# A fixed order for the opening of a hybrid decoder layer: one k-tile first, first modulation on TensorE, a closing norm over three engines

## The chip, the core and the metric

The kernel runs on one core of one Trainium2 chip. The metric is the device time of one execution in microseconds. The engines are TensorE (PE, its weight loads PEld), VectorE (DVE), ScalarE (ACT), GpSimd (POOL) and SyncE (SP), which issues most transfers.

## What is computed

x is 256 tokens by 2048 channels, float32; c is one conditioning vector. The reference, cut:

```
mod = silu(c) @ w_ada + b_ada            # w_ada 2048 x 6144
shift, scale, gate = split(mod, 3)
h = layer_norm(x) * (1 + scale) + shift
proj = h @ w_in                          # 2048 x 9280
q_lat, kv_lat, mla_gate, pool_in, pool_gate, gate_logits = split(proj)
y_mla = (mla(q_lat, kv_lat) * silu(mla_gate)) @ w_mla_o
y_pool = (pool(pool_in) * silu(pool_gate)) @ w_pool_o
g_mla, g_pool = split(sigmoid(gate_logits + b_gates), 2)
y = (g_mla * y_mla + g_pool * y_pool) @ w_out
out = layer_norm(ALPHA * x + (1 + gate) * y, ln_g, ln_b)
```

The first layer norm has no weights. No product with w_in can start before the shift and the scale of its 128 input channels are known, and each of these is a sum over all 2048 rows of w_ada.

## The kernel before

Products keep float32 accuracy by splitting both operands: hi is the operand rounded by a ScalarE copy, lo the rest, subtracted on VectorE (`split`, lines 92 to 94), and a block's product is three matmuls, hi by hi, lo by hi and hi by lo (`mm3t`, lines 104 to 106). Weights arrive as raw tiles of up to 1 MB (five buffers, `RAWB`) and are converted into hi/lo pairs of 128x1024 (four pairs, `HB`). A job is one such pair and its matmuls: two k-tiles of 128 channels for one block of 512 columns and both halves of the tokens, 12 matmuls of 512 columns. `execute` writes the jobs out in order, with conversions up to four pairs ahead; a planner (the tile framework's scheduler) then orders the instructions of each engine by priority and by its own estimate of when they are ready, and sets the waits.

The 2048 channels are 16 k-tiles. w_in has 18 blocks of 512 columns for the token-major branches (qkv 2, pi 2, pg 2, gp 4, mg 4, gm 4). It is worked through in four groups of k-tiles, `KGROUPS`: 2, 4, 4 and 6. In each group all blocks get their partial product; the first group's is copied from PSUM by ScalarE (line 453), later ones are added by VectorE to the stored tile (line 455). One exception, `early_jobs`: the qkv blocks take k-tiles 0 and 1 one after the other, as soon as each is modulated.

The modulations (`ada_jobs`) stand between these jobs, placed by `weave` over the first 85% of a group. For a set of k-tiles, VectorE multiplies each of 16 slices of w_ada by a column of silu(c) and sums (`accumulate`, lines 323 and 325); TensorE then folds the 128 partitions by a product with a column of ones (line 350), VectorE adds the bias (354, 357), ScalarE applies shift and scale to the normalised, transposed x (363) and splits it into hh and hl. The sets are 1, 1, 2, 2, 4, 2 and 4 k-tiles. A sum over one k-tile has 128x256 steps, over two 128x512, over four 128x1024.

At the start x (2 MB) is loaded, its statistics taken on VectorE (406), it is normalised by ScalarE (423), transposed by TensorE (432) and copied back (435). At the end, the last block of the last projection is done for the first 128 tokens, then for the others in two halves of 256 columns (`out_mm`, 955 to 957), each followed by `residual` on VectorE (930 to 933). `closing_norm` centres four pieces of 512 columns on VectorE (940); for the first tokens ScalarE scales and GpSimd adds the bias (945, 946), for the last ones VectorE does both in one step (948).

Of the kernel before, what the change touches and what calls it, by code (L numbers as in the profile page):

```python
# [15 lines left out]
P = 128  # L16
# [21 lines left out]
SPL = 0  # L38
# [19 lines left out]
KGROUPS = ((0, 2), (2, 4), (6, 4), (10, 6))  # L58
# [3 lines left out]
def hybrid_layer(  # L62
# [222 lines left out]
    vT = const.tile([P, 80], F32, name="vT")  # L285
    VB_ADA, VB_G, VB_PS, VB_Q, VB_KV = 0, 32, 64, 72, 76

    def load_vecs():
        for o, n, src in (
            (VB_ADA, 32, b_ada[0, 0:2 * D]), (VB_G, 32, b_gates[0]), (VB_PS, 8, pool_scale[0]),  # L290
            (VB_Q, 4, q_norm_g[0]), (VB_KV, 4, kv_norm_g[0]),
        ):
            nc.sync.dma_start(vecs[o:o + n, :], src.rearrange("(r q) -> r q", q=P))
# [22 lines left out]
    def accumulate(accs, raw, per, ui):  # L316
        w = accs[0].shape[1]
        for i in range(per):
            t = ui * per + i
            src = raw[:, i * w:(i + 1) * w]  # L320
            acc = accs[t % len(accs)]
            if t < len(accs):
                V.tensor_scalar(acc, src, s_c[:, t:t + 1], None, op0=ALU.mult)
            else:
                V.scalar_tensor_tensor(acc, src, s_c[:, t:t + 1], acc, op0=ALU.mult, op1=ALU.add)  # L325

    def ada_jobs(k0, nk):
# [5 lines left out]
        def unit(raw, ui):  # L333
            if ui == 0:
                acc = ck(shape=(P, 1024), name="acc") if nk > 2 else wk(512, "acc")
                accs.extend(acc[:, o * 2 * ncol:(o + 1) * 2 * ncol] for o in range(2 if nk == 1 else 1))
            accumulate(accs, raw, per, ui)
# [8 lines left out]
        def finish():  # L346
            pa = bank()
            for j in range(2 * nk):
                for i, acc in enumerate(accs):
                    T.matmul(  # L350
                        pa[:, j:j + 1], lhsT=acc[:, j * P:(j + 1) * P], rhs=ones[:, 0:1], start=i == 0,
                        stop=i == len(accs) - 1,
                    )
            V.tensor_tensor(
                mod_shift[:, k0:k0 + nk], pa[:, 0:nk], vT[:, VB_ADA + k0:VB_ADA + k0 + nk], op=ALU.add,
            )
            V.scalar_tensor_tensor(
                mod_scale[:, k0:k0 + nk], pa[:, nk:2 * nk], 1.0,
                vT[:, VB_ADA + KT + k0:VB_ADA + KT + k0 + nk], op0=ALU.add, op1=ALU.add,
            )  # L360
# [17 lines left out]
    def rstd_steps(dst, var, eps, ve, t):  # L378
        def a():
            V.tensor_scalar(ve, var, eps, None, op0=ALU.add)  # L380
            A.activation(t, ve, AF.Sqrt)
            V.reciprocal(dst, t)
# [16 lines left out]
    norms = []  # L399

    def input_norm():
        load_vecs()
        for t in range(2):
            st = work.tile([P, 4, 6], F32, tag="bns", name="bns")
            for j in range(4):
                V.bn_stats(st[:, j, :], xt[2 * t + j // 2][:, (j % 2) * 512:(j % 2 + 1) * 512])
            mu, rs = ln_stats(st)
            nmr = work.tile([P, 1], F32, tag="nmr", name="nmr")
            V.tensor_scalar(nmr, mu, rs, -1.0, op0=ALU.mult, op1=ALU.mult)
            norms.append((rs, nmr))  # L410
        normalize(0)
        pv = bank()
        T.transpose(pv[:, :P], vecs, ident)
        A.copy(vT, pv[:, :80])
        to_features(0, 2)
        normalize(1)
        to_features(2, 4)

    def normalize(j):
        for t in range(2):  # L420
            rs, nmr = norms[t]
            xx = xt[2 * t + j]
            A.activation(xx, xx, AF.Identity, scale=rs, bias=nmr)

    def to_features(q0, q1):
        for q in range(q0, q1):
            nT.append(ck(name="nT"))
            for t in range(2):
                pt = bank()
                for j in range(4):  # L430
                    k = q * 4 + j
                    T.transpose(
                        pt[:, j * P:(j + 1) * P], xt[2 * t + k // 8][:, (k % 8) * P:(k % 8 + 1) * P], ident,
                    )
                A.copy(nT[q][:, :, t * P:(t + 1) * P], pt.rearrange("p (j n) -> p j n", j=4))
# [42 lines left out]
    def early_jobs(name):  # L478
        banks = []

        def fn(wh, wl, k):
            if k == 0:
                banks.extend(bank() for _ in range(4))
            xh, xl = hsl(hh, k), hsl(hl, k)
            for t in range(2):
                ts = slice(t * P, (t + 1) * P)
                for cb in range(2):
                    cs = slice(cb * CB, (cb + 1) * CB)
                    mm3t(banks[2 * t + cb], xh[:, ts], xl[:, ts], wh[:, 0, cs], wl[:, 0, cs], k == 0, k == 1)
# [366 lines left out]
    def gate_jobs(cb):  # L856
        accs = []

        def unit(raw, ui):
# [3 lines left out]
            accumulate(accs[:1], raw, 4, ui)  # L863
# [71 lines left out]
    def closing_norm(t):  # L935
        mu, rs = ln_stats(fin["s"][t])
        order = (0, 1, 2, 3)
        for j in order:
            uc = fin["u"][t][j // 2][:, j % 2, :]
            V.scalar_tensor_tensor(uc, uc, mu, fin["g"][j // 2][:, j % 2, :], op0=ALU.subtract, op1=ALU.mult)  # L940
        for j in order:
            uc = fin["u"][t][j // 2][:, j % 2, :]
            bc = fin["b"][j // 2][:, j % 2, :]
            if t == 0 or j < SPL:
                A.activation(uc, uc, AF.Copy, scale=rs)
                G.tensor_tensor(uc, uc, bc, op=ALU.add)
            else:
                V.scalar_tensor_tensor(uc, uc, rs, bc, op0=ALU.mult, op1=ALU.add)
            nc.sync.dma_start(out[t * P:(t + 1) * P, j * 512:(j + 1) * 512], uc)
# [9 lines left out]
    def out_jobs(cb):  # L959
# [3 lines left out]
        def fn(wh, wl, kc, kh):  # L963
# [10 lines left out]
            if last:  # L974
                residual(0, cb, banks[0])
                if cb < 3:
                    residual(1, cb, banks[1])
                else:
                    closing_norm(0)
                    for q in range(2):  # L980
# [121 lines left out]
```

## Time and profile before

| | |
|---|---|
| median of 3 runs | 803.99 us (803.51 to 804.83) |
| the profiled execution's own time | 803.81 us |
| its span, first to last instruction | 802.0 us |
| TensorE busy | 767.5 us (96%) |
| VectorE busy | 649.7 us (81%) |
| ScalarE busy | 422.7 us (53%) |
| moved by DMA | 195.41 MB |

The span leaves out what lies around the instructions, 1.8 us here. Matmuls are pipelined, so a busy TensorE counts overlapping instructions once; start-to-start times tell its rate. The clock granted to TensorE is given as a share of full speed: 1.00 or 0.50 at a moment, in between as a mean over a stretch.

### The profile page before, as it was taken

Reading aid. Unit: us, or ns where it says so; the run is one execution under the profiler, and the core shown is the slowest. Engines: PE = TensorE matmul, PEld = TensorE weight load, DVE = VectorE, ACT = ScalarE, POOL = GpSimd, SP = SyncE. Lnnn points to the kernel's source line nnn. Section 1 sums busy time; section 2 is a strip of 40 time slices with the busy share of each in tenths; the row PEclk is TensorE's granted clock in tenths of the full one; section 3 lists DMA queues with packets and bytes.
Section 4 is the critical chain, followed back from the end, with each engine's and each line's share of the span. In section 5 each row is a group of like instructions: output and inputs, shape, how many; then the busy total and the mean of one; then the engine's idle time right before and its main releaser. Section 6 shows DMA issues by size and latency. Waiting matters only on the chain.

```text
span 802.0 us, 10653 instructions
## 1 busy us (share of the span) xinstructions
PE 767.5 (96%) x3985; PEld 658.6 (82%) x3985; DVE 649.7 (81%) x977; ACT 422.7 (53%) x588; POOL 12.0 (2%) x51
## 2 busy tenths in 40 slices
PE   2699999999999999999999999999999999999993
PEld 2588888888888888888888999999998888888883
DVE  6978798979998886678978769887776899769855
ACT  5467643353433556565665676666664344443611
POOL 1000000000000000000100000000000000000002
PEclk9799999999999999999999999999999999999997
DMA  9999998968998666645766646556454979789502
GB/s 284 328 309 363 375 354 299 343 214 280 332 343 300 218 216 198 208 132 178 256 222 188 193 145 197 200 196 200 161 196 121 318 272 343 266 323 362 206 2 105
DMA packets 112989, 195.41 MB, mean 244 GB/s; under 512 B 6484, under 2 KB 32292, under 8 KB 112936
## 3 DMA queue, kind: packets, MB, share of 16 engines
q1 hardware_dynamic: 112296, 192.62, 71.4%
q0 software_dynamic: 640, 2.10, 0.9%
q8 instruction: 31, 0.51, 0.3%
q14 instruction: 22, 0.18, 0.1%
HBM read 192.60 MB, written 2.10 MB: 243 GB/s over the span
## 4 chain that ended last, share of the span: by engine, by line
PE 94%; DMA 3%; DVE 2%; SPq 1%; ACT 0%; issue 0%; DVEq 0%; ACTq 0%
PE ps L104 22%; PE ps L106 22%; PE ps L105 22%; PE ps L957 4%; PE ps L956 4%; PE ps L955 4%; PE ps L98 2%; PE ps L97 2%; PE ps L99 2%; PE ps L260 2%; PE ps L832 1%; DMA raw<-in_w_ada_dram 1%; PE ps L759 1%; PE ps L758 1%; PE ps L760 1%; DMA raw<-in_w_in_dram 1%
## 5 line engine op out<-in xcount | busy, mean ns | idle before, releaser
L93 ACT ACTIVATE hi<-raw 128x1024 fp32r<-128x1024 f32 (+1 forms) x256 | 267.0, 1044 | 299.5 <-PE ps L105 201.5
L94 DVE TENSOR_TENSOR lo<-raw,hi 128x1024 fp32r<-128x1024 f32 x254 | 304.8, 1203 | 82.2 <-ACT hi L93 81.6
L104 PE MATMUL ps<-hi,hh 128*128 128x512 f32 x576 | 225.9, 396 | 4.8 <-ACT hh L93 3.6
L105 PE MATMUL ps<-hi,hl 128*128 128x512 f32 x576 | 225.9, 392 | 0.0
L106 PE MATMUL ps<-lo,hh 128*128 128x512 f32 x576 | 221.8, 392 | 0.0
L325 DVE SCALAR_TENSOR_TENSOR acc<-raw,s_c,acc 128x512 f32<-128x512 f32 (+2 forms) x163 | 128.5, 798 | 16.8 <-DMA raw<-in_w_ada_dram 15.0
L104 PEld LDWEIGHTS ps<-hi,hh 128*128 128x128 f32 x576 | 109.4, 190 | 27.4 <-ACT hh L93 3.8
L106 PEld LDWEIGHTS ps<-lo,hh 128*128 128x128 f32 x576 | 109.2, 190 | 23.0
L105 PEld LDWEIGHTS ps<-hi,hl 128*128 128x128 f32 x576 | 109.3, 190 | 22.7 <-DVE hl L94 0.4
L104 PE MATMUL ps<-hi,zh 128*128 128x512 f32 x128 | 50.2, 397 | 0.0
L105 PE MATMUL ps<-hi,zl 128*128 128x512 f32 x128 | 50.2, 392 | 0.0
L106 PE MATMUL ps<-lo,zh 128*128 128x512 f32 x128 | 49.4, 391 | 0.0
L97 PE MATMUL ps<-cn_h,hi 128*128 128x256 f32 x160 | 46.0, 288 | 0.0
L98 PE MATMUL ps<-cn_l,hi 128*128 128x256 f32 x160 | 45.2, 283 | 0.0
L99 PE MATMUL ps<-cn_h,lo 128*128 128x256 f32 x160 | 45.2, 283 | 0.0
L957 PE MATMUL ps<-hi,ml 128*128 128x512 f32 (+1 forms) x120 | 45.1, 376 | 0.0
L956 PE MATMUL ps<-lo,mh 128*128 128x512 f32 (+1 forms) x120 | 45.0, 375 | 0.0
L955 PE MATMUL ps<-hi,mh 128*128 128x512 f32 (+1 forms) x120 | 44.9, 376 | 0.0
L98 PEld LDWEIGHTS ps<-cn_l,hi 128*128 128x128 f32 x160 | 30.6, 191 | 0.1
L97 PEld LDWEIGHTS ps<-cn_h,hi 128*128 128x128 f32 x160 | 30.6, 191 | 0.1
L99 PEld LDWEIGHTS ps<-cn_h,lo 128*128 128x128 f32 x160 | 30.6, 191 | 0.0
L106 PEld LDWEIGHTS ps<-lo,zh 128*128 128x128 f32 x128 | 24.0, 188 | 5.1
(211 smaller groups left out, 991.8 us busy)
## 6 DMA issues: line engine op xcount, KB each, us to landing
raw<-in_w_in_dram SPq DMA_DIRECT2D x55, 1024.0 KB, 5.8
raw<-in_w_ada_dram SPq DMA_DIRECT2D x64, 512.0 KB, 6.5
raw<-in_w_in_dram SPq DMA_DIRECT2D x35, 512.0 KB, 3.8
raw<-in_w_ada_dram SPq DMA_DIRECT2D x16, 1024.0 KB, 5.8
raw<-in_w_mla_o_dram SPq DMA_DIRECT2D x16, 1024.0 KB, 5.2
raw<-in_w_out_dram SPq DMA_DIRECT2D x16, 1024.0 KB, 5.7
raw<-in_w_kv_b_dram SPq DMA_DIRECT2D x8, 1024.0 KB, 5.4
raw<-in_w_pool_o_dram SPq DMA_DIRECT2D x8, 1024.0 KB, 5.0
```

Of the source, the lines that this page charges most:

```text
L93: A.activation(hi, src, AF.Copy)
L94: V.tensor_tensor(lo, src, hi.bitcast(F32), op=ALU.subtract)
L97: T.matmul(ps, lhsT=wh, rhs=xh, start=first, stop=False, skip_group_check=True)
L98: T.matmul(ps, lhsT=wh, rhs=xl, start=False, stop=False, skip_group_check=True)
L99: T.matmul(ps, lhsT=wl, rhs=xh, start=False, stop=last, skip_group_check=True)
L104: T.matmul(ps, lhsT=xh, rhs=wh, start=first, stop=False, skip_group_check=True)
L105: T.matmul(ps, lhsT=xl, rhs=wh, start=False, stop=False, skip_group_check=True)
L106: T.matmul(ps, lhsT=xh, rhs=wl, start=False, stop=last, skip_group_check=True)
L325: V.scalar_tensor_tensor(acc, src, s_c[:, t:t + 1], acc, op0=ALU.mult, op1=ALU.add)
L955: T.matmul(ps, lhsT=xh, rhs=wh[:, k, :], start=first and k == 0, stop=False)
L956: T.matmul(ps, lhsT=xh, rhs=wl[:, k, :], start=False, stop=False)
L957: T.matmul(ps, lhsT=xl, rhs=wh[:, k, :], start=False, stop=last and k == 1)
```

## The change

Way in. `way_in` replaces `input_norm`, `early_jobs` and the first two modulations, and together with the jobs of the first k-group it runs under `manual_schedule`, in which TensorE, VectorE, ScalarE and SyncE keep the order of the program. The sum for k-tile 0 is done on TensorE: for 13 of the 16 slices of w_ada, `direct` uses the slice as stationary operand and one column of silu(c) as the moving one; slices 3, 7 and 11 stay on VectorE. For k-tile 1, slices 0 to 13 are on VectorE, 14 and 15 on TensorE. Eight blocks (qkv, pi, pg and the first two of gp) take k-tile 0 alone, in four pairs; qkv keeps its four PSUM banks until k-tile 1 is modulated, the others are copied out. The transposes of x stand between the products of `direct`. Normalising is split between ScalarE and VectorE. Four small loads go out from ScalarE instead of five from SyncE.

k-groups. After that: ten blocks take k-tiles 0 and 1; then six take 1 to 3 and twelve 2 and 3; then all 18 take 4 to 7; then all take 8 to 15. The modulation sets are 2, 4, and 4 and 4, woven into the first three of these.

End. The first tokens' closing norm is wholly on VectorE. Of the last tokens' first piece, 448 columns are made on TensorE as three products added in PSUM: the identity by the bias, a diagonal of the root by the residual (already multiplied by the weight), a diagonal of minus mean times root by the weight. ScalarE copies it out. VectorE's steps go piece by piece, one of them between the root's request and its use; the end is under `manual_schedule` for VectorE and ScalarE.

The diff, cut:

```diff
+TE = 448
-KGROUPS = ((0, 2), (2, 4), (6, 4), (10, 6))
...
+            nc.scalar.dma_start(vecs[o:o + n, :], src.rearrange("(r q) -> r q", q=P))
...
+    def fold(pa, acc, first, last):
+        n = acc.shape[1] // P
+        for j in range(n):
+            T.matmul(pa[:, j:j + 1], lhsT=acc[:, j * P:(j + 1) * P], rhs=ones[:, 0:1], start=first and j == 0,
+                     stop=last, skip_group_check=True)
...
-            V.tensor_tensor(t, dst, dst, op=ALU.mult)
-            V.tensor_tensor(t, t, ve, op=ALU.mult)
+                V.scalar_tensor_tensor(t, dst, dst, ve, op0=ALU.mult, op1=ALU.mult)
...
+        def direct(pa, r, t, first, last):
+            for j in range(2):
+                T.matmul(pa[:, j:j + 1], lhsT=r[:, t % 8, j, :], rhs=s_c[:, t:t + 1], start=first and j == 0,
+                         stop=last, skip_group_check=True)
+        def apply(k, pa):
+            modulation(pa, k, 1)
+            h = wk(S, "h")
+            A.activation(hsl(hh, k), hsl(nT, k), AF.Identity, scale=mod_scale[:, k:k + 1], bias=mod_shift[:, k:k + 1])
+            V.tensor_scalar(h, hsl(nT, k), mod_scale[:, k:k + 1], mod_shift[:, k:k + 1], op0=ALU.mult, op1=ALU.add)
+            V.tensor_tensor(hsl(hl, k), h, hsl(hh, k).bitcast(F32), op=ALU.subtract)
+        def product(pair, k, banks, first, last):
+            xh, xl = hsl(hh, k), hsl(hl, k)
+            for cb in range(2):
+                cs = slice(cb * CB, (cb + 1) * CB)
+                for t in range(2):
+                    ts = slice(t * P, (t + 1) * P)
+                    mm3t(banks[2 * cb + t], xh[:, ts], xl[:, ts], pair[0][:, cs], pair[1][:, cs], first, last)
...
+        load_vecs()
+        w_q = w_load(0, OFFS["qkv"], 2 * CB)
+        r0 = [ada_load(0, u) for u in range(2)]
+        w_p = w_load(0, OFFS["pi"], 4 * CB)
+        w_g = w_load(0, OFFS["gp"], 2 * CB)
+        r1 = [ada_load(1, 0)]
+        w_q1 = w_load(1, OFFS["qkv"], 2 * CB)
+        r1.append(ada_load(1, 1))
...
+        to_features(0)
+        pq = convert(w_q)
...
+        pa, acc = bank(), wk(2 * P, "acc")
+        for t in range(16):
+            if t in (4, 8, 12):
+                to_features(t // 4)
+            if t == 12:
+                fold(pa, acc, False, False)
+            if t in (3, 7, 11):
+                accumulate(acc, r0[t // 8][:, t % 8].rearrange("p s n -> p (s n)"), t, t == 3)
+            else:
+                direct(pa, r0[t // 8], t, t == 0, t == 15)
+        apply(0, pa)
+        pp = [convert(w_p[:, i * HALF:(i + 1) * HALF]) for i in range(2)]
+        bq = [bank() for _ in range(4)]
+        product(pq, 0, bq, True, False)
+        pg = convert(w_g)
+        for pair, name in ((pp[0], "pi"), (pp[1], "pg"), (pg, "gp")):
+            banks = [bank() for _ in range(4)]
+            product(pair, 0, banks, True, True)
+            if name == "pg":
+                accumulate_1(0, 8)
+                pq = convert(w_q1)
+            evict(name, 0, banks)
+        accumulate_1(8, 14)
+        pa = bank()
+        fold(pa, acc, True, False)
+        for t in (14, 15):
+            direct(pa, r1[1], t, False, t == 15)
+        apply(1, pa)
+        product(pq, 1, bq, False, True)
+        evict("qkv", 0, bq)
...
+    def closing_norm_1():
+        V.bn_aggr(mv[:, 0:2], fin["s"][1].rearrange("p a b -> p (a b)"))
+        a, b = rstd_steps(rs, mv[:, 1:2], LN_EPS, ve, t)
+        T.matmul(ps[:, :TE], lhsT=ident, rhs=part("b", 1, 0, 0, TE), start=True, stop=False, skip_group_check=True)
+        a(lambda: centre(1, 1, mu))
+        b()
+        V.tensor_scalar(nmr, mu, rs, -1.0, op0=ALU.mult, op1=ALU.mult)
+        for i, (sc, src) in enumerate(((rs, "u"), (nmr, "g"))):
+            d = dg[:, i * P:(i + 1) * P]
+            A.activation(d, ident, AF.Copy, scale=sc)
+            T.matmul(ps[:, :TE], lhsT=d, rhs=part(src, 1, 0, 0, TE), start=False, stop=i == 1, skip_group_check=True)
+        A.copy(part("u", 1, 0, 0, TE), ps[:, :TE])
+        put(1, 0, 0, TE)
+        close(1, 1, rs)
+        for j, c0 in ((2, 0), (3, 0), (0, TE)):
+            centre(1, j, mu, c0)
+            close(1, j, rs, c0)
...
+    fixed = tc.manual_schedule(engines={getattr(mybir.EngineType, e) for e in ("PE", "DVE", "Activation", "SP")})
+    fixed.__enter__()
+    way_in()
+    names = ("pi", "pg", "gp", "qkv", "mg", "gm")
+    ahead = (("pi", 0), ("pi", 1), ("pg", 0), ("pg", 1), ("gp", 0), ("gp", 1))
+    def groups(n, cb):
+        if (n, cb) in ahead:
+            return None, (1, 3), (4, 4), (8, 8)
+        return None if n == "qkv" else (0, 2), (2, 2), (4, 4), (8, 8)
+    ADA = (((2, 2),), ((4, 4),), ((8, 4), (12, 4)))
...
+        if gi == 0:
+            main += todo(lambda: fixed.__exit__(None, None, None), rope_load)
```

## Rows read from the trace of the kernel before

**Rows 1.** The page's first part: busy us, share, instructions.

```profile
PE 767.5 (96%) x3985; PEld 658.6 (82%) x3985; DVE 649.7 (81%) x977; ACT 422.7 (53%) x588; POOL 12.0 (2%) x51
```

**Rows 2.** Busy time by stretch: length, PE, PEld, DVE, ACT, POOL, clock, DMA share, GB/s.

```profile
38.00:84.00 46.00, 46.00 (x199) 38.05 (x200) 37.64 (x49) 33.32 (x53) 1.23 (x2) 0.94 1.00 343
84.00:186.00 102.00, 102.00 (x459) 84.74 (x458) 89.92 (x100) 45.42 (x50) 0.00 (x0) 1.00 0.88 308
186.00:286.00 100.00, 100.00 (x454) 83.20 (x454) 91.89 (x110) 43.02 (x44) 0.54 (x1) 1.00 0.87 297
```

**Rows 3.** Waits of TensorE, whole execution: us in total, times, longest.

```profile
PE ps L104 <- ACT hh L93: 3.6, 1, 3.6
```

**Rows 4.** Timeline of TensorE in the stream: start, length; twelfth product after the first.

```profile
774.65 0.39 PE L955 MATMUL ps<-hi,mh 128*128 128x512 f32 x1
...
777.15 0.39 PE L957 MATMUL ps<-hi,ml 128*128 128x512 f32 x1
```

**Rows 5.** Timeline of TensorE, way in: start, length of the merged row.

```profile
13.64 1.12 PE L432 MATMUL ps<-ident,x 128*128 128x128 f32 x4 [2.21 <-ACT x L423]
16.66 4.79 PE L432 MATMUL ps<-ident,x 128*128 128x128 f32 x28 [1.90 <-ACT x L423]
21.30 0.95 PE L350 MATMUL ps<-ones,acc 128*128 128x1 f32 x8
25.80 1.40 PE L104 MATMUL ps<-hi,hh 128*128 128x512 f32 x4 [3.55 <-ACT hh L93]
...
35.35 1.27 PE L350 MATMUL ps<-ones,acc 128*128 128x1 f32 x6
...
42.75 0.63 PE L105 MATMUL ps<-hi,hl 128*128 128x512 f32 x1
...
43.60 0.45 PE L105 MATMUL ps<-hi,hl 128*128 128x512 f32 x1
```

**Rows 6.** Timeline of VectorE and ScalarE, way in.

```profile
17.74 3.25 DVE L325 SCALAR_TENSOR_TENSOR acc<-raw,s_c,acc 128x256 f32<-128x256 f32 x8 [0.43 <-DMA raw<-in_w_ada_dram]
...
25.33 0.42 ACT L93 ACTIVATE hh<-nT 128x256 fp32r<-128x256 f32 x1
...
28.86 1.06 ACT L93 ACTIVATE hi<-raw 128x1024 fp32r<-128x1024 f32 x1 [3.11 <-DMA raw<-in_w_in_dram]
...
46.25 0.59 ACT L494 COPY qkv<-ps 128x512 f32<-128x512 f32 x1
```

**Rows 7.** Timeline of VectorE while its queue is full.

```profile
63.61 3.10 DVE L325 SCALAR_TENSOR_TENSOR acc<-raw,s_c,acc 128x512 f32<-128x512 f32 x4
66.63 1.22 DVE L94 TENSOR_TENSOR lo<-raw,hi 128x1024 fp32r<-128x1024 f32 x1
...
103.82 1.28 DVE L455 TENSOR_TENSOR pi<-ps,pi 128x512 f32<-128x512 f32 x2
105.02 1.21 DVE L94 TENSOR_TENSOR lo<-raw,hi 128x1024 fp32r<-128x1024 f32 x1
106.15 1.27 DVE L325 SCALAR_TENSOR_TENSOR acc<-raw,s_c,acc 128x1024 f32<-128x1024 f32 x1
107.35 1.21 DVE L94 TENSOR_TENSOR lo<-raw,hi 128x1024 fp32r<-128x1024 f32 x1
```

**Rows 8.** Waits from 186 to 260 us: us in total, times, longest.

```profile
ACT hi L93 <- PE ps L105: 43.3, 26, 2.3
```

**Rows 9.** Timeline: a float32 product in attention, then the end.

```profile
494.70 0.83 PE L832 MATMUL ps<-vn,pT 128*128 128x128 f32 x6
...
783.79 0.42 DVE L932 SCALAR_TENSOR_TENSOR ua<-ua,tmp 128x256 f32<-128x256 f32 x1
...
788.77 0.28 PE L957 MATMUL ps<-hi,ml 128*128 128x256 f32 x1
...
789.54 1.52 DVE L932 SCALAR_TENSOR_TENSOR ua<-ua,tmp 128x256 f32<-128x256 f32 x1
...
795.55 2.74 DVE L948 SCALAR_TENSOR_TENSOR ua<-ua,mv,lb 128x512 f32<-128x512 f32 x4
```

More of the change, by code (lines that the diff above doesn't have):

```diff
@@ L37 @@
 NW = 8
-SPL = 0
+TE = 448
 WA = (0.0, 0.0, 0.0, 0.0)
@@ L314, in hybrid_layer, with accumulate, accumulate_raw, modulation @@
     nT, hh, hl = [], [], []
-    def accumulate(accs, raw, per, ui):
-        w = accs[0].shape[1]
-        for i in range(per):
[L319 to L325, printed above, removed]
+    def accumulate(acc, src, t, first):
+        if first:
+            V.tensor_scalar(acc, src, s_c[:, t:t + 1], None, op0=ALU.mult)
+        else:
+            V.scalar_tensor_tensor(acc, src, s_c[:, t:t + 1], acc, op0=ALU.mult, op1=ALU.add)
+    def accumulate_raw(acc, raw, per, ui):
+        w = acc.shape[1]
+        for i in range(per):
+            accumulate(acc, raw[:, i * w:(i + 1) * w], ui * per + i, ui == i == 0)
+    def modulation(pa, k0, nk):
+        V.tensor_tensor(
+            mod_shift[:, k0:k0 + nk], pa[:, 0:nk], vT[:, VB_ADA + k0:VB_ADA + k0 + nk], op=ALU.add,
+        )
+        V.scalar_tensor_tensor(
+            mod_scale[:, k0:k0 + nk], pa[:, nk:2 * nk], 1.0,
+            vT[:, VB_ADA + KT + k0:VB_ADA + KT + k0 + nk], op0=ALU.add, op1=ALU.add,
+        )
+    def fold(pa, acc, first, last):
+        n = acc.shape[1] // P
+        for j in range(n):
+            T.matmul(
+                pa[:, j:j + 1], lhsT=acc[:, j * P:(j + 1) * P], rhs=ones[:, 0:1], start=first and j == 0,
+                stop=last, skip_group_check=True,
+            )
     def ada_jobs(k0, nk):
@@ L347, in finish @@
             pa = bank()
[L348 to L360, printed above, removed]
+            fold(pa, accs[0], True, True)
+            modulation(pa, k0, nk)
             for k in range(k0, k0 + nk):
@@ L397, in ln_stats, with normalize, to_features @@
         return mv[:, 0:1], mv[:, 2:3]
-    norms = []
-    def input_norm():
-        load_vecs()
+    def normalize(t, a, b, scale_bias):
+        rs, nmr = scale_bias
+        xx = xt[2 * t + a // HALF][:, a % HALF:a % HALF + b - a]
+        if a < HALF:
+            A.activation(xx, xx, AF.Identity, scale=rs, bias=nmr)
+        else:
+            V.tensor_scalar(xx, xx, rs, nmr, op0=ALU.mult, op1=ALU.add)
+    def to_features(q):
+        nT.append(ck(name="nT"))
         for t in range(2):
-            st = work.tile([P, 4, 6], F32, tag="bns", name="bns")
+            pt = bank()
             for j in range(4):
[L406 to L435, printed above, removed]
+                k = q * 4 + j
+                T.transpose(
+                    pt[:, j * P:(j + 1) * P], xt[2 * t + k // 8][:, (k % 8) * P:(k % 8 + 1) * P], ident,
+                )
+            A.copy(nT[q][:, :, t * P:(t + 1) * P], pt.rearrange("p (j n) -> p j n", j=4))
     def hsl(tiles, k):
@@ L933, in residual, with part @@
         V.bn_stats(fin["s"][t][:, cb if si is None else si, :], uc)
[L935 to L949, printed above, removed]
+    def part(name, t, j, c0=0, c1=512):
+        w = fin[name][t][j // 2] if name == "u" else fin[name][j // 2]
+        return w[:, j % 2, c0:c1]
@@ L974, in fn @@
             if last:
[L975 removed]
                 if cb < 3:
+                    residual(0, cb, banks[0])
                     residual(1, cb, banks[1])
[L978 to L986 removed]
+                    if cb == 0:
+                        u = part("u", 1, 0, 0, TE)
+                        V.tensor_tensor(u, u, part("g", 1, 0, 0, TE), op=ALU.mult)
+                else:
+                    with tc.manual_schedule(engines={mybir.EngineType.DVE, mybir.EngineType.Activation}):
+                        residual(0, cb, banks[0])
+                        closing_norm_0()
+                        for q in range(2):
+                            c0, c1 = 256 * q, 256 * q + 256
+                            ps = bank()
+                            for kc, kh, wh, wl, first, last in keep:
+                                out_mm(ps[:, :256], 1, kc, 2 * kh, wh[:, :, c0:c1], wl[:, :, c0:c1], first, last)
+                            residual(1, cb, ps, c0, c1, 3 + q)
+                        closing_norm_1()
         jobs = []
```

167 lines of the change are left out of this document (106 added, 61 removed).

## The prediction, made before the result was known

> **What bounds the kernel now.** I read the page's busy shares first. TensorE is busy for 767.5 of 802.0 us and VectorE for 649.7 [rows 1], so the time is TensorE's work plus what it waits for. The table by stretch then says where. From 38 us on TensorE is busy in every stretch without a break, while VectorE is busy for 37.6 of 46, 89.9 of 102 and 91.9 of 100 us [rows 2]: these are the stretches in which the input projection goes on while the modulations are still being summed. TensorE's own list of waits has five entries, all before 38 us; one is 3.6 us for the first modulated k-tile [rows 3]. The change can therefore win only ahead of the continuous stream and behind TensorE's last product, and it can lose where VectorE, at about 90%, is given more to do per microsecond of TensorE.
>
> A 512-column product takes 0.227 us in the stream: 11 steps from 774.65 to 777.15 [rows 4]. At the lower of the two clock levels it takes 0.426 (two from 42.75 to 43.60 [rows 5]). From the first of them at 25.80 to 43.60 TensorE does 34 such products, with gaps and at the lower clock [rows 5]. 34 x 0.227 is 7.7, so the stream runs as if it had begun at 35.9 and never paused. I call this the effective start; the change replaces it.
>
> **The new way in: effective start 33.9, gain 2.0.** The order is now that of the program on TensorE, VectorE, ScalarE and SyncE. x and its statistics stay, so I let the transposes of x begin at 13.6 as before (13.64 [rows 5]). The five loads of small vectors become four, moved from SyncE's queue to ScalarE's: small ones, issued sooner than before, when SyncE issued them behind x. ScalarE's copy of them now stands ahead of its two roots; before, both were over by 13.64, and they are if the loads land no later than they did. That I cost at nothing; each us of delay there would shift the whole way in by one.
> From 13.6 TensorE has, in a fixed row, 32 transposes at 4.79/28 = 0.17 us [rows 5], 5.5; 13 x 2 one-column products in place of VectorE's sums, two instructions each, 0.24 a product (eight instructions in 0.95 [rows 5]), 6.2; and 0.5 for the three sums left on VectorE. That is 12.2, to 25.8. Two small VectorE steps add the bias, and ScalarE applies both (0.42 [rows 6]): 0.8 with hand-overs, so the first real product at 26.6. Before it was 25.80 [rows 5]: the sums left VectorE for an engine that must also transpose. Bounds. The weights must land: before, the second half of the first modulation had landed at 17.74 [rows 6]; 0.5 MB of projection weights now stands ahead of it, 1.5 us at 0.34 MB/us [rows 2], then the last eight products (1.9) and 0.8: 22.0. At the lower clock a one-column product costs 0.42 (six instructions in 1.27 [rows 5]): 13.6 + 5.5 + 11 + 0.9 + 0.8 = 31.8. I take 26.6.
> Then four pairs of blocks at k-tile 0 are 48 products without a gap. Three things cost time afterwards. Gap A: six one-column products (1.4), then 0.8 as above: 2.2 before k-tile 1, since nothing else stands there on TensorE. Its weights are there long before (8.5 MB from the start, 25 us at 0.34 MB/us). Gap B: the next blocks' conversions stand on ScalarE behind the eviction of the last bank, so 0.59 for it, 1.06 for hi [rows 6], 1.21 for lo [rows 7], less 0.45 for the two products that need only hi, and 0.2 for hand-overs: 2.6. Clock: before, the first 46 us of the stream had a mean granted clock of 0.94 [rows 2], 2.8 us lost to the lower level after gaps of this kind; bounds 0 and twice that, 5.6, for two gaps; I take 2.5. Sum: 26.6 + 2.2 + 2.6 + 2.5 = 33.9 against 35.9. Ends: 26.8 and 42.2.
>
> **The new k-groups: VectorE becomes the bound, +8.** Before, groups of 2, 4, 4 and 6 k-tiles; now 2, 2, 4 and 8, so that all sums but the last group's must be done by k-tile 8 instead of 10. VectorE's steps, start to start in a full queue: the lo half of 128x1024 1.135 (105.02 to 106.15), adding a block's two banks 1.20 (103.82 to 105.02), a 128x1024 sum 1.20 (106.15 to 107.35), a 128x512 sum 0.755 (four from 63.61 to 66.63) [rows 7]. Do these add up? From 84 to 286 before: 72 conversions 81.7, 36 blocks 43.2, sums 19.2 + 12.1 + 19.2, the modulated tiles and the first rope steps some 6: 181.4. Measured 89.9 + 91.9 = 181.8 [rows 2].
> Now by group. First (ten blocks, k-tiles 0 and 1): TensorE 120 x 0.227 + 1 = 28.2; VectorE ten conversions 11.4, sixteen 128x512 sums 12, 0.8: 24.2. No stall.
> Second (six blocks of k-tiles 1 to 3, twelve of 2 and 3): TensorE 252 products 57.2 + eight foldings 1.9 = 59.1. VectorE 18 full and 6 half conversions 24.0, 18 blocks 21.6, sixteen 128x1024 sums 19.2, the modulated tile 1.1: 65.9.
> Third (18 blocks, k-tiles 4 to 7): TensorE 432 products 98.1 + 3.8 = 101.9. VectorE 40.9 + 21.6 + 32 sums 38.4 + 2.3 = 103.2.
> So VectorE has 169.1 for TensorE's 161.0: 8.1 over. Four hi/lo pairs let it be three conversions ahead at the start (-3.5). The sums are woven into the first 85% of a group, so in the last 5.4 jobs of the third VectorE has 9.4 for TensorE's 14.7 and the 5.3 left over come too late (+5.3). Some 1.9 of adds can still be owed at that point. That gives 8. Before, the same count for the third group gives 96 against 101: no stall, as seen; ScalarE waited 43.3 us in 74 for TensorE to free a hi [rows 8], so conversions were ahead. Bounds: 2, if the planner lets sums slide into that last 15%; 14, if VectorE is busy only 96% of the time because of waits for weights (the third group moves 35 MB in 102 us, 0.34 MB/us, what 38 to 84 us moved before [rows 2]). The fourth group has VectorE to spare, but time lost by TensorE is not made up.
> The Trainium skill, page Perfetto Trace Analysis, section Identifying the Most-Contended Engine, finds the bottleneck by occupancy: the engine with the highest share is the one to improve. By that, VectorE at 81% [rows 1] is not the bound and this term is 0, which is the first rival; the table by stretch shows 90% where it matters, and that is the one I go by.
>
> **The closing norm: -1.2.** Behind TensorE's last product the chain is VectorE's. Its residual step took 1.52 us where the same step took 0.42 when GpSimd was idle [rows 9]; GpSimd's four adds are gone: -1.1. Of eight full steps of 0.68 (four in 2.74 [rows 9]) behind the last product, 448 columns' worth of two move to TensorE and ScalarE, one centring fills the wait for the root, one small step is dropped: about -1.0. Against that, the output strip made on TensorE needs two plain f32 products of 448 columns: 0.83/3 x 3.5 = 0.97 each at full clock, 1.9 at the lower [rows 9], behind the scale, which is ready some 3.5 us after the last product; with its copy it ends 6 to 8 us after it, where VectorE by my count ends at 7.1 (before 9.2: 798.29 - 789.05 [rows 9]). If SyncE issues the outputs in program order, four stores at some 0.4 queue behind that strip. Ends -2.1 and -0.3; I take -1.2. The first half's eight steps on VectorE end about 1 us before the last residual needs it; without that cover each us late is a us.
>
> **Sum.** The profiled execution took 803.81 us (span 802.0, 1.8 around it), 0.18 below the median shown. 803.81 - 2.0 + 8 - 1.2 = 808.6.
>
> **Rivals.** (1) VectorE's excess is absorbed: sums slide, or the planner orders them behind conversions. For it: no wait of TensorE for VectorE after 38 us before [rows 3]. Against it: 169.1 does not go into 161.0. With a stall of 0 it gives 800.6; the kernel is measurably faster while the stall is under 3.2 - 1.6 = 1.6 and measurably slower once it is over 4.8; this is the rival of the other sign, and VectorE's excess decides it. (2) The way in is bound by the transfers and not by TensorE's row, start at 22.0 and a steady clock: effective start 26.8, 803.81 - 9.1 - 1.2 + 8 = 801.5. For it: such products can start while later weights land. Against: 12.2 us of TensorE's work would have to fit between 13.6 and 21.2. (3) The one-column products keep the lower clock: start 42.2, so 803.81 + 6.3 - 1.2 + 8 = 817. For it: they ran at 0.42 a product at 35.35 [rows 5]; against: at 0.24 right after the transposes.
>
> **Numbers.** Forecast 0.48, rival 1 0.26, rival 2 0.14, rival 3 0.12. 0.2% is 1.6 us, about what a measurement of this kernel can tell from no change. Faster by more: most of rivals 1 and 2, 0.36. Within: their upper ends and the forecast's lower, 0.12. Slower: 0.52. The forecast's own range is 804 to 813. For 8 in 10, rival 1 with an early start (796) to the lower part of rival 3 (815).
>
> **What would show it.** Right: between some 65 and 225 us VectorE at 97% or more, TensorE with many short gaps put down to lo of the conversion line, ScalarE no longer waiting for TensorE there; first product at 26 to 27.5; two gaps of 2 to 3 us before 50. Wrong: TensorE at 100% through that stretch (rival 1), a first product at 22 to 23 (rival 2) or past 30 (rival 3). A last VectorE step later than 8 us behind the last product would refute the closing term.

## The result, and the profile after

The changed kernel takes 840.13 us (median of three executions, 838.9 to 841.0) where before takes 803.9: 1.0447 times as long, 95% interval 1.0427 to 1.0468. A fourth execution took 1566.5 us and is left out; with it the median is 840.58, from which the expectations below count. The forecast had the sign and one of its mechanisms, but 808.6 (796 to 815) is far too little. The profiled execution took 841.03, its span is 838.9; before's span was 802.0, so 36.9 us have to be found.

The page's first part, after; [rows 1] answer to it.

```profile
PE 795.9 (95%) x4043; PEld 679.1 (81%) x4043; DVE 648.0 (77%) x951; ACT 421.4 (50%) x586; POOL 7.0 (1%) x47
```

TensorE is busy for 28.4 us more with the same products, and VectorE for no longer than before: the first sign that TensorE ran slower, not only that it waited. The table by stretch (length, then busy time of PE, PEld, DVE, ACT, POOL, then clock, DMA share, GB/s), beside [rows 2]:

```profile
14.00:34.00 20.00, 18.91 (x88) 18.36 (x88) 4.86 (x11) 8.44 (x14) 0.00 (x0) 1.00 0.68 205
50.00:62.00 12.00, 9.82 (x27) 6.79 (x28) 6.12 (x8) 7.28 (x11) 0.54 (x1) 0.72 0.52 147
91.70:163.30 71.60, 63.05 (x257) 50.76 (x257) 65.12 (x77) 25.85 (x29) 0.00 (x0) 0.90 0.84 282
163.30:222.00 58.70, 52.82 (x223) 43.74 (x222) 55.78 (x60) 21.55 (x23) 0.00 (x0) 0.92 0.98 343
```

Before, TensorE had no gap after 38 us. Now it has gaps up to 213 us, and from there it runs to the last product of the matrix work without one. Its waits from 40 to 290 us (total, times, longest), beside [rows 3]:

```profile
PE ps L339 <- DVE acc L319: 12.3, 3, 5.9
PE ps L103 <- ACT hi L92: 4.4, 4, 1.6
PE ps L103 <- ACT h L92: 1.8, 1, 1.8
PE ps L103 <- ACT h L504: 1.0, 1, 1.0
PE ps L105 <- DVE lo L93: 0.5, 1, 0.5
```

L339 is the folding: the matmuls that turn VectorE's sums `acc` into a modulation. The many short gaps put down to `lo` did not come; two long ones at the folding did. Of the prediction's other signs, a VectorE at 97% came between the holds only, and ScalarE did not stop waiting for TensorE. VectorE from 160 to 200 us, then ScalarE's waits from 60 to 290 us:

```profile
160.00:200.00 40.00, 40.00 (x178) 33.13 (x177) 39.94 (x43) 15.21 (x15) 0.00 (x0) 1.00 0.95 328
...
ACT hi L92 <- PE ps L104: 63.5, 41, 3.0
ACT hi L92 <- DMA raw<-in_w_in_dram: 43.8, 17, 5.9
```

The second of ScalarE's waits is for weights. That is a rival cause of TensorE's gaps; e7 below decides it.

**The way in.** TensorE's timeline, beside [rows 5]:

```profile
14.03 2.34 PE L422 MATMUL ps<-ident,x 128*128 128x128 f32 x8 [5.75 <-ACT x L412]
16.16 2.56 PE L496 MATMUL ps<-s_c,raw 128*128 128x1 f32 x12
18.70 1.97 PE L422 MATMUL ps<-ident,x 128*128 128x128 f32 x8
...
29.50 3.55 PE L496 MATMUL ps<-s_c,raw 128*128 128x1 f32 x16
34.05 0.79 PE L103 MATMUL ps<-hi,h 128*128 128x512 f32 x1 [1.01 <-ACT h L504]
...
38.05 0.39 PE L103 MATMUL ps<-hi,h 128*128 128x512 f32 x1
...
50.02 0.49 PE L103 MATMUL ps<-hi,h 128*128 128x512 f32 x1 [0.95 <-ACT h L504]
...
56.21 0.49 PE L103 MATMUL ps<-hi,h 128*128 128x512 f32 x1 [1.63 <-ACT hi L92]
...
57.47 0.51 PE L105 MATMUL ps<-lo,h 128*128 128x512 f32 x1 [0.53 <-DVE lo L93]
...
61.92 0.39 PE L105 MATMUL ps<-lo,h 128*128 128x512 f32 x1
```

From 14.03 to 33.04 TensorE is never idle. Twelve one-column instructions take 2.54 us to the next row (0.21 each, 0.42 a product) and eight transposes 1.75 (0.22): the rate of the lower level throughout, and the first nine real products, until 38.05, are at it too. The first comes at 34.05. 74 products have begun before 61.92, from where the rate is full: 61.92 - 74 x 0.227 = 45.1 is the effective start, where before had 35.9. **The way in costs 9.2 us.**

**The stream.** The last product of the matrix work starts at 826.32, before at 788.77 [rows 9]: 37.55 later, 9.2 of it from the way in. **28.3 us are lost between 62 and 222 us.** One of the two long holds, on three engines:

```profile
143.25 0.39 PE L105 MATMUL ps<-lo,h 128*128 128x512 f32 x1
144.07 0.68 DVE L445 TENSOR_TENSOR mg<-ps,mg 128x512 f32<-128x512 f32 x1
...
144.67 1.21 DVE L93 TENSOR_TENSOR lo<-raw,hi 128x1024 fp32r<-128x1024 f32 x1
145.80 1.28 DVE L445 TENSOR_TENSOR gm<-ps,gm 128x512 f32<-128x512 f32 x2
...
147.00 1.21 DVE L93 TENSOR_TENSOR lo<-raw,hi 128x1024 fp32r<-128x1024 f32 x1
148.13 1.27 DVE L319 SCALAR_TENSOR_TENSOR acc<-raw,s_c,acc 128x1024 f32<-128x1024 f32 x1
...
149.46 3.57 PE L339 MATMUL ps<-ones,acc 128*128 128x1 f32 x16 [5.83 <-DVE acc L319]
...
152.89 0.77 PE L103 MATMUL ps<-hi,h 128*128 128x512 f32 x1
153.07 0.16 DVE L327 TENSOR_TENSOR mod_shift<-ps,vT 128x4 f32<-128x4 f32 x1 [2.22 <-PE ps L339]
...
155.84 0.69 DVE L445 TENSOR_TENSOR gm<-ps,gm 128x512 f32<-128x512 f32 x1 [2.54 <-PE ps L105]
...
157.61 0.39 PE L105 MATMUL ps<-lo,h 128*128 128x512 f32 x1
```

TensorE takes its instructions in order. At 143.6 the next one is the folding, and the last sum it needs stands on VectorE behind two conversions and three halves of a block's addition; it is done at 149.4. The conversions are for products that stand behind the folding, and the additions store products already made. Then the folding itself takes 3.43 us to the next row where 16 such instructions at the full rate take 1.70 (e9 below, 152.85 to 154.55), eleven products take 4.72 where 2.50 would do, and VectorE, late until now, waits 2.22 and 2.54 us for TensorE. At 207 us the same happens for k-tiles 8 to 11: 5.88 us idle, folding 3.43, 14 products in 6.07 for 3.18.

After 85 us the list of waits leaves 16.3 us (its total less what lies at 47, 50 and 56 us). The lower rate behind three of the gaps adds 1.7 at 91.67, 1.7 + 2.2 at 149 and 1.7 + 2.9 at 212: 10.2. Together 26.5 of the 28.3; the rest is open.

**The end**, beside [rows 9]:

```profile
826.32 0.28 PE L1091 MATMUL ps<-hi,ml 128*128 128x256 f32 x1
...
827.10 0.43 DVE L1035 SCALAR_TENSOR_TENSOR ua<-ua,tmp 128x256 f32<-128x256 f32 x1
...
830.42 1.86 PE L1077 MATMUL ps<-ua,dg 128*128 128x448 f32 x2 [3.06 <-ACT dg L1076]
...
833.63 0.53 ACT L1078 COPY ua<-ps 128x448 f32<-128x448 f32 x1 [2.97 <-PE ps L1077]
833.91 0.28 DVE L1051 SCALAR_TENSOR_TENSOR ua<-ua,mv,lb 128x64 f32<-128x64 f32 x1
```

The residual step takes 0.43 in place of 1.52. VectorE ends 7.9 us behind the start of the last product (9.5 before), but the span ends 4.7 us after VectorE (3.7 before): 12.58 for 13.23, **0.65 us gained**. 9.2 + 28.3 - 0.65 = 36.9.

### The profile page after: what moved, and what is told of

Same layout as the page of the kernel before. It is cut to its first block, busy times and chain, and to the rows that moved or that the text cites. A ratio compares the mean times of both kernels' runs of the same rounds, so it can differ in the third digit from the quotient of the medians.

```text
span 838.9 us, 10749 instructions
## 1 busy us (share of the span) xinstructions
PE 795.9 (95%) x4043; PEld 679.1 (81%) x4043; DVE 648.0 (77%) x951; ACT 421.4 (50%) x586; POOL 7.0 (1%) x47
## 4 chain that ended last, share of the span: by engine, by line
PE 83%; DVE 9%; DMA 3%; issue 2%; ACT 1%; SPq 0%; DVEq 0%; ACTq 0%
PE ps L103 18%; PE ps L104 18%; PE ps L105 18%; PE ps L1091 3%; PE ps L1090 3%; PE ps L1089 3%; DVE lo L93 3%; DVE acc L319 3%; PE ps L97 2%; PE ps L96 2%; PE ps L98 2%; DMA raw<-in_w_ada_dram 2%; PE ps L259 1%; PE ps L496 1%; PE ps L935 1%
## 5 line engine op out<-in xcount | busy, mean ns | idle before, releaser
L93 DVE TENSOR_TENSOR lo<-raw,hi 128x1024 fp32r<-128x1024 f32 (+1 forms) x257 | 305.3, 1191 | 109.1 <-ACT hi L92 104.8
L103 PE MATMUL ps<-hi,hh 128*128 128x512 f32 x432 | 170.1, 394 | 0.0
L104 PE MATMUL ps<-hi,hl 128*128 128x512 f32 x432 | 169.2, 392 | 0.0
L105 PE MATMUL ps<-lo,hh 128*128 128x512 f32 x432 | 165.7, 391 | 0.0
L105 PEld LDWEIGHTS ps<-lo,hh 128*128 128x128 f32 x432 | 81.8, 189 | 17.2
L104 PEld LDWEIGHTS ps<-hi,hl 128*128 128x128 f32 x432 | 81.9, 189 | 16.8
L103 PEld LDWEIGHTS ps<-hi,hh 128*128 128x128 f32 x432 | 81.8, 189 | 16.7
L103 PE MATMUL ps<-hi,h 128*128 128x512 f32 x144 | 60.2, 421 | 8.1 <-ACT hi L92 4.4
L104 PE MATMUL ps<-hi,h 128*128 128x512 f32 x144 | 59.6, 414 | 0.0
L105 PE MATMUL ps<-lo,h 128*128 128x512 f32 x144 | 55.5, 413 | 0.5 <-DVE lo L93 0.5
L1091 PE MATMUL ps<-hi,ml 128*128 128x512 f32 (+1 forms) x120 | 45.1, 376 | 0.0
L103 PEld LDWEIGHTS ps<-hi,h 128*128 128x128 f32 x144 | 28.8, 200 | 17.0 <-ACT hi L92 6.7
```

The lines of the kernel that those rows point to most:

```text
L93: V.tensor_tensor(lo, src, hi.bitcast(F32), op=ALU.subtract)
L103: T.matmul(ps, lhsT=xh, rhs=wh, start=first, stop=False, skip_group_check=True)
L104: T.matmul(ps, lhsT=xl, rhs=wh, start=False, stop=False, skip_group_check=True)
L105: T.matmul(ps, lhsT=xh, rhs=wl, start=False, stop=last, skip_group_check=True)
L1091: T.matmul(ps, lhsT=xl, rhs=wh[:, k, :], start=False, stop=last and k == 1)
```

## The experiments

Each ratio is to runs of the kernel before on the same chip (medians 803.97 to 804.48).

| run | median us | ratio to before, 95% interval |
|---|---|---|
| e1_groups_alone | 832.05 | 1.0342 (1.0326 to 1.0357) |
| e2_closing_alone | 802.87 | 0.9986 (0.9977 to 0.9995) |
| e3_sums_early | 848.27 | 1.0554 (1.0536 to 1.0571) |
| e4_sums_on_vector | 829.92 | 1.0323 (1.0302 to 1.0344) |
| e5_products_first | 839.77 | 1.0443 (1.0418 to 1.0468) |
| e6_fold_later | 839.52 | 1.0443 (1.0408 to 1.0479) |
| e7_half_sums | 816.71 | 1.0148 (1.0123 to 1.0173) |
| e8_five_groups | 829.63 | 1.0319 (1.0276 to 1.0363) |
| e9_fill_holds | 832.86 | 1.0348 (1.0327 to 1.0368) |
| e10_vector_five | 819.72 | 1.0198 (1.0176 to 1.0221) |
| e11_all_on_vector | 831.71 | 1.0351 (1.0317 to 1.0384) |
| e12_no_strip | 803.41 | 0.9989 (0.9980 to 0.9998) |

**The parts alone: e1 and e2.** e1 is the kernel before with

```diff
-KGROUPS = ((0, 2), (2, 4), (6, 4), (10, 6))
+KGROUPS = ((0, 2), (2, 2), (4, 4), (8, 8))
...
-    ADA = ((0, 1), (1, 1), (2, 2), (4, 2), (6, 4), (10, 2), (12, 4))
+    ADA = ((0, 1), (1, 1), (2, 2), (4, 4), (8, 4), (12, 4))
```

> The kernel before with nothing but the new k-groups (2, 2, 4 and 8 k-tiles) and the new split of the sums. Theory A (the forecast's: only VectorE's surplus of work is lost): the second group has 62.3 us of VectorE's work for 51 of TensorE's, the third 103.2 for 101.9, less 3.5 for conversions that are ahead: 812 to 818 us, TensorE's gaps short and put down to lo of the conversion line. Theory B (TensorE is held up in its fixed order by a folding whose last sum VectorE has not yet made, and loses again at the lower clock behind each hold): two holds of 4 to 6 us put down to acc, the lower clock behind them, 825 to 832 us. Theory C (the loss after 85 us comes from the new way in, not from the groups): 804 us.

832.05: 28.1 us from the k-groups alone, what the trace of the whole change gives for the stream (28.3). Theory C falls, and so does the size of theory A; the two holds of theory B are there, longer than it said. The two foldings, in TensorE's timeline:

```profile
142.76 3.57 PE L350 MATMUL ps<-ones,acc 128*128 128x1 f32 x16 [7.37 <-DVE acc L325]
...
249.99 3.58 PE L350 MATMUL ps<-ones,acc 128*128 128x1 f32 x16 [6.66 <-DVE acc L325]
```

e2 is the kernel before with the new `closing_norm_0`, `closing_norm_1`, `rstd_steps` and the fixed order in `out_jobs`, and nothing else.

> The kernel before with nothing but the new closing norm. The forecast's term: 1.2 us less, 802.7. As read from the two profiles (12.3 us behind the last main product in place of 12.95): 0.65 less, 803.3. If the whole closing gain was only the quiet of GpSimd: 1.1 less, and the strip on TensorE buys nothing. In every case the end stays within 2 us of before.

802.87, 1.1 less than its 803.98. Parts: 9.2 (from the trace) + 28.1 - 1.1 = 36.2, and the whole change cost 36.2 (840.13 - 803.91): they add.

**Where VectorE's surplus goes: e3, e6, e7, e8, e9.** e3 is the changed kernel with

```diff
-WB = (0.85, 0.85, 0.85, 0.8)
+WB = (0.85, 0.6, 0.6, 0.8)
```

> The changed kernel with the sums of the second and third group woven into the first 60% of the group's jobs in place of the first 85%. Theory A (VectorE's surplus is lost wherever it stands): VectorE has the same work, the conversions wait in place of the foldings, 836 to 843 us. Theory B (holds at the folding): the sums are over before the folding comes up, the two waits for acc of 5.9 us and the lower clock behind them go, some of it comes back as waits for lo: 815 to 828 us.

848.27: worse than either theory. The sums packed closer push the conversions back (waits for `lo` and `hi` 10.5 us), and the folding still waits, 6.33 us:

```profile
206.74 3.57 PE L339 MATMUL ps<-ones,acc 128*128 128x1 f32 x16 [6.33 <-DVE acc L319]
```

e6 moves one folding only:

```diff
+            if gi == 2:
+                ada[1][6:6] = ada[0][-1:]
+                del ada[0][-1]
```

> The changed kernel with one job moved: the folding of k-tiles 8 to 11, which no product needs before the fourth group, stands at 0.71 of the third group's jobs in place of 0.43. VectorE's work is the same. Theory A (VectorE's surplus is lost wherever TensorE stands): the time comes back as waits for lo or hi, 838 to 842 us. Theory B (TensorE's fixed order with the folding ahead of ready products): the hold of 5.9 us at 207 and the lower clock of the folding and the products behind it (about 4 us) go, 830 to 834 us.

839.52: unchanged. The hold at 207 us is gone and has come back at the third group's last folding:

```profile
257.10 3.57 PE L339 MATMUL ps<-ones,acc 128*128 128x1 f32 x16 [5.16 <-DVE acc L319]
```

So theory B, the order by itself, falls: it decides only where TensorE stands and waits. That TensorE waits is VectorE's surplus, as in theory A. e7 takes the surplus away:

```diff
-        for i in range(per):
+        for i in range(1 if w == 1024 else per):
```

> The changed kernel with every second one of the 128x1024 sums left out (24 of 48, so the second half of the modulations is not the reference's); all loads stay. VectorE has 29 us less to do between 50 and 260 us. If VectorE's surplus is what TensorE's holds come from: no hold over 1 us after 85 us, 840.6 - 28 = 812 us. If the weights' transfers behind the modulation's loads set it: the conversions still wait for weights, 825 us or more.

816.71, 23.4 less than the changed kernel, and from 85 to 290 us TensorE waits only twice, 0.7 and 1.0 us. The time is 4.7 above the 812 expected, which these two waits do not cover; the rest is open. It is not the weights' arrival: the loads are the same, and from 85 to 290 us ScalarE waits as long for weights (37.7 us, in the changed kernel 35.4) without TensorE waiting for it. The stretch from 85 to 222 us, first the changed kernel, then e7:

```profile
85.00:222.00 137.00, 120.75 (x504) 98.27 (x503) 126.08 (x144) 53.39 (x62) 0.00 (x0) 0.91 0.91 314
```

```profile
85.00:222.00 137.00, 135.29 (x615) 111.97 (x614) 119.78 (x142) 61.14 (x71) 0.00 (x0) 1.00 1.01 362
```

TensorE is at 135.3 of 137 and at the full clock once VectorE has room; the transfers move more, not less. e8 gives the third group half of its sums to a fourth group:

```diff
-            return None, (1, 3), (4, 4), (8, 8)
-        return None if n == "qkv" else (0, 2), (2, 2), (4, 4), (8, 8)
+            return None, (1, 3), (4, 4), (8, 4), (12, 4)
+        return None if n == "qkv" else (0, 2), (2, 2), (4, 4), (8, 4), (12, 4)
...
-    ADA = (((2, 2),), ((4, 4),), ((8, 4), (12, 4)))
+    ADA = (((2, 2),), ((4, 4),), ((8, 4),), ((12, 4),))
...
```

> The changed kernel with five k-groups, 2, 2, 4, 4 and 4, in place of four: the sums of k-tiles 8 to 11 have the third group to themselves and those of 12 to 15 the fourth; 18 more blocks are added up (21.6 us of VectorE's work). By the counts of work: VectorE has 84 us for the third group's 102 and for the fourth's 100, so only the second group's surplus of 7 is left: one hold, at the folding of k-tiles 4 to 7, 824 to 832 us. If the holds come whatever the load, 838 to 842 us.

829.63, 10.5 less than the changed kernel and as the count of work says, with a single hold, 6.08 us at 147, in the one group that still has a surplus; and that although VectorE has 21.6 us more to do in all. e9 leaves VectorE as it is and gives TensorE something to do:

```diff
             pa = bank()
+            for _ in range(26 if k0 in (4, 8) else 0):
+                T.matmul(pa, lhsT=ones_r, rhs=hh[0][:, 0:2, :].rearrange("p a n -> p (a n)"), start=True, stop=True)
             fold(pa, accs[0], True, True)
```

> The changed kernel with 26 useless 512-column products (5.9 us at the full rate; their result is overwritten) in TensorE's order somewhat ahead of the folding of k-tiles 4 to 7, and 26 ahead of that of 8 to 11: TensorE has work in place of each hold of 5.9 us. If behind each hold the lower clock costs some 4 us more (folding and ten products at the lower rate, VectorE waiting for them): no idle time at the foldings, the clock stays up, 831 to 834 us although there is more work. If a hold costs only its own idle time: 839 to 842 us.

832.86: 7.3 us faster with 11.8 us of useless work. The same stretch, e9, and its first folding:

```profile
85.00:222.00 137.00, 130.99 (x581) 105.97 (x580) 128.67 (x146) 54.08 (x62) 0.00 (x0) 0.99 0.92 321
...
152.85 1.84 PE L339 MATMUL ps<-ones,acc 128*128 128x1 f32 x16
154.55 0.49 PE L104 MATMUL ps<-hi,h 128*128 128x512 f32 x1
```

The clock is 0.99 where it was 0.91, no folding in this stretch waits, and both take 1.70 to the next row. What lies behind a hold (3.9 and 4.6 us by the trace) therefore comes with the hold and is a price beside its idle time. The 7.3 us do not measure that price alone: the planner also put the first folding some 23 products later, and by the traces e9 was 2.7 us ahead before its first useless product, as the wait at 91 us was shorter (0.73 for 1.81) and the full rate followed it.

**The way in: e4, e5, e11.** e4:

```diff
-            if t == 12:
-                fold(pa, acc, False, False)
-            if t in (3, 7, 11):
-                accumulate(acc, r0[t // 8][:, t % 8].rearrange("p s n -> p (s n)"), t, t == 3)
+            if t not in (0, 1, 4, 8, 12, 13):
+                accumulate(acc, r0[t // 8][:, t % 8].rearrange("p s n -> p (s n)"), t, t == 2)
             else:
-                direct(pa, r0[t // 8], t, t == 0, t == 15)
+                direct(pa, r0[t // 8], t, t == 0, False)
+        fold(pa, acc, False, True)
```

> The changed kernel with 10 of the first modulation's 16 sums on VectorE and 6 on TensorE (before: 3 and 13), the folding behind the last of them. If TensorE's row of one-column products sets the first product: its row shrinks by 7 x 0.42 = 2.9 us, and as VectorE, idle for 11.1 us there, needs about 10 x 0.45 us from 20.6 on, the first product comes at 30 to 31.5 in place of 34.05 and the kernel at 837 to 838. If the weights' landing sets it: first product unchanged, 840.6.

829.92, 10.2 less: far more than expected. One error was mine: a sum on TensorE is two products, so seven fewer save 7 x 2 x 0.42 = 5.9, not 2.9. The first product comes 5.3 us earlier:

```profile
28.74 0.79 PE L103 MATMUL ps<-hi,h 128*128 128x512 f32 x1 [1.01 <-ACT h L504]
```

109 products have begun before 61.95, an effective start of 61.95 - 109 x 0.227 = 37.2, 7.9 earlier. 5.3 is the row of one-column products; most of the rest is that the two gaps behind the first blocks, of the same length (3.1 and 2.5 us), are not followed by the lower clock here. The other 2 us lie in the stream: TensorE's waits from 85 to 290 us are 14.3 us in place of 16.3.

e5:

```diff
         A.copy(vT, pv[:, :48])
+        pw = bank()
+        for _ in range(24):
+            T.matmul(pw[:, :P], lhsT=ones, rhs=ones, start=True, stop=True)
```

> The changed kernel with 24 extra products of 128x128 (ones by ones, into a bank that nobody reads) on TensorE in the idle time ahead of x's transposes. If the one-column products and transposes are slow because TensorE came out of idle at the lower level: 0.24 a one-column product and 0.17 a transpose as before, first product at 27 to 29, 830 to 834 us. If they hold the lower level themselves, whatever ran ahead of them: 0.42 and 0.22 again, first product at 34, 840 us.

839.77, beside 840.13: nothing gained. TensorE's timeline:

```profile
15.68 1.04 PE L422 MATMUL ps<-ident,x 128*128 128x128 f32 x8
16.55 1.40 PE L496 MATMUL ps<-s_c,raw 128*128 128x1 f32 x12
19.10 1.82 PE L422 MATMUL ps<-ident,x 128*128 128x128 f32 x8 [1.15 <-ACT x L412]
20.70 2.56 PE L496 MATMUL ps<-s_c,raw 128*128 128x1 f32 x12
...
34.30 0.79 PE L103 MATMUL ps<-hi,h 128*128 128x512 f32 x1 [1.01 <-ACT h L504]
```

The full rate is there at first: 0.11 a transpose, 0.117 a one-column instruction, twelve in 1.40. It is lost again by 20.70 and does not return until real products run. So the idle time ahead of the transposes is not what keeps the rate low. Whether TensorE lost it at the wait of 1.15 us ahead of 19.10 or by what it ran does not show here; from 20.70 to 33.3 it is never idle and stays at the lower rate. e11 has no one-column products in the first modulation:

```diff
-            if t in (3, 7, 11):
-                accumulate(acc, r0[t // 8][:, t % 8].rearrange("p s n -> p (s n)"), t, t == 3)
-            else:
-                direct(pa, r0[t // 8], t, t == 0, t == 15)
+            accumulate(acc, r0[t // 8][:, t % 8].rearrange("p s n -> p (s n)"), t, t == 0)
+        fold(pa, acc, True, True)
```

> The changed kernel with all 16 sums of the first modulation on VectorE, so that TensorE has only x's transposes and the folding ahead of the first product. VectorE: 16 sums of about 0.45 us from 20.6 on end at 27.8 or later, folding and hand-over 1.8: first product at 29.5 to 31, later than with 10 sums on VectorE (28.74). The transposes should run at 0.17 us each if it is the one-column products that keep the clock low, at 0.22 if they do not. Time 829 to 833 us.

831.71, first product at 30.89, as expected. The transposes:

```profile
18.73 5.07 PE L422 MATMUL ps<-ident,x 128*128 128x128 f32 x24 [2.33 <-ACT x L412]
```

0.21 each: here they run at the lower rate without any one-column product beside them. They need not: in before, the row of 28 transposes of [rows 5] ends at the full rate, 0.11 each, so its mean of 0.17 is a mixture of both levels:

```profile
20.97 0.49 PE L432 MATMUL ps<-ident,x 128*128 128x128 f32 x3
21.30 0.95 PE L350 MATMUL ps<-ones,acc 128*128 128x1 f32 x8
```

Of the three splits run, the middle one is best: 13 sums on TensorE give the first product at 34.05, none 30.89, six 28.74.

**Together, and the strip: e10, e12.** e10 is e4 with e8's five groups.

> The two repairs together: 10 of the first modulation's sums on VectorE and five k-groups (2, 2, 4, 4, 4). If the way in and the groups' holds are separate losses, the gains add: 840.6 - 10.7 - 10.9 = 819 us. If the faster way in only brings TensorE sooner to a VectorE that is the bound there: 824 to 830 us.

819.72, 20.4 less than the changed kernel, and the two alone gave 10.2 and 10.5: way in and holds are separate losses. It is still 15.7 us above before: the hold at k-tiles 4 to 7 (4.89 us) and the gaps behind the first blocks remain. e12 is e2 without TensorE's part (cut; the first of the three products and the strip's earlier product with the weight go too):

```diff
-        for i, (sc, src) in enumerate(((rs, "u"), (nmr, "g"))):
-            d = dg[:, i * P:(i + 1) * P]
-            A.activation(d, ident, AF.Copy, scale=sc)
-            T.matmul(ps[:, :TE], lhsT=d, rhs=part(src, 1, 0, 0, TE), start=False, stop=i == 1, skip_group_check=True)
-        A.copy(part("u", 1, 0, 0, TE), ps[:, :TE])
-        put(1, 0, 0, TE)
-        for j, c0 in ((2, 0), (3, 0), (0, TE)):
+        for j in (2, 3, 0):
```

> The kernel before with the new closing norm less its TensorE part: all four strips of the second half on VectorE, GpSimd still idle. If the gain of the closing norm alone (803.98 to 802.87) comes from GpSimd's quiet: 802.5 to 803.0, as VectorE's 1.1 us more (two steps of 448 columns at about 0.65, less 0.2) is given back by stores that start sooner. If the strip on TensorE carries it: 803.8 to 804.2.

803.41 beside 804.45, ratio 0.9989; e2's is 0.9986. The strip on TensorE and ScalarE buys nothing that can be measured: in the traces VectorE ends 7.9 us behind the start of the last product with it and 8.7 without, but the span ends 4.7 and 4.1 us behind VectorE. GpSimd's quiet fits as the gain, as the residual step takes 0.42 in both in place of 1.52; no run changes it alone, and both also have the new order of VectorE's steps. Of all versions, these two alone are faster than before, by about 0.1%.

## Why the prediction was wrong, step by step

| term | forecast | measured |
|---|---|---|
| way in | -2.0 | +9.2 (trace) |
| k-groups | +8 | +28.3 (trace), +28.1 (e1) |
| closing norm | -1.2 | -0.65 (trace), -1.1 (e2) |

**The way in failed in the price of the row on TensorE.** The forecast took 0.24 for a one-column product and put 0.42 at the end of the range. All 26 cost 0.42: 10.9 us for 6.2. The transposes cost 7.4 for 5.5. With a start 0.4 later, the folding 0.2 and the hand-over 0.25 more that is 34.05 for 26.6. The 0.24 came from eight instructions right behind 28 transposes, whose rate had risen by then (e11); I took the level of that row as that of the kind of instruction. Gap A was 3.1 for 2.2, gap B 2.5 for 2.6, the lower clock and what is left 5.4 for 2.5. Rival 3 named this case and priced the first product at 31.8; it had 0.12. Rival 2 is refuted by the table and the timeline: between 14 and 34 us the transfers stand at 0.68, and TensorE has no wait from 14.03 to 33.04.

**The k-groups: mechanism right, size 28 for 8.** VectorE as the bound is right: e7 shows it, rival 1 falls, and the count of work was good (65.9 us for the second group, 65.1 busy in it). Three things made the size wrong. First, the two credits, 3.5 for conversions that are ahead and 1.9 for additions still owed: without them the forecast's own sum is 13.4, and the second and third group lost 14.5 in waits; that neither credit existed fits this but has no run of its own, and the closeness is in part luck: 5.3 of the 13.4 was put at the end of the third group, where the folding at 260.01 does not wait. Second, the price of a gap: the clock was charged in the way in, to gaps of 2 us, and not to the stall. It adds 10.2 us by the trace; e9, with two gaps filled, was 7.3 us faster, though not by this alone. Third, VectorE does not use the time behind a hold: it waits 4.8 us for the slow folding and products (149.6 to 155.8), so that the second group lasts 71.6 us with 65.1 of work. Where the stall shows was also wrong: at `acc` of the folding, not at `lo`.

The Trainium skill, page Perfetto Trace Analysis, section Identifying the Most-Contended Engine, takes VectorE by its busy share and judges TensorE's headroom by the busy share of its weight loads (or by its rate of arithmetic), not by that of its matmuls: 77% and 81% here, so it would still name TensorE. The same page's section Optimization Strategy says that the most contended engine can change from one regime to the next. e7 agrees with the second: 29 us less on VectorE gave 23.4 us.

**The closing norm** was right in size by e2, and its terms come out near. GpSimd's quiet is 1.1 at the residual step. The steps moved to TensorE let VectorE end 0.8 earlier (e2 against e12), and the stores behind them give 0.6 of it back, so that nothing is left that can be measured; the forecast had named those stores as what stands against the strip.

## What to carry to other kernels

Count a group's work on every engine between two points that no work can pass, as here, but price each gap that TensorE gets as the gap plus the products at the lower rate behind it, and be slow to take off credits for slack that the trace of the old schedule shows. A small step on an engine that works in order is as late as the last input it names, and all that stands behind it is as late too; where the engine that feeds it has more work than time, moving that step moves the wait and does not pay it (e6). Before work is moved to TensorE in one-column pieces, price it at the lower level too, as all 26 products here ran at it.

## What the runs showed of the hardware

- TensorE busy without a break for 19 us (14.03 to 33.04) with transposes and one-column products ran at the lower rate all that time, and stayed there for four more us of 512-column products. In e5 it had the full rate at 16.55 and had lost it by 20.70, with a wait of 1.15 us between. In e11, 24 transposes in a row stayed at the lower rate; in before, 28 in a row ended at the full one. What decides it stays open.
- The granted-clock column is 1.00 for 14 to 34 us of the changed kernel while every row there has the lower rate; in e5, with the same rows at the same rate from 20.70 on, it is 0.64 for the same stretch. The column did not tell the rate there; the durations did.
- With 11.8 us of useless products put in, the kernel was 7.3 us faster (e9).
- Two gaps of 3.1 and 2.5 us were followed by the lower clock in the changed kernel (0.72 from 50 to 62 us) and not in e4 (1.00). What decides it stays open.
